# Hybrid DiT step: layer 0's first products by quarters of the contraction, partial sums in SBUF

## The chip, the core and the metric

One core of a Trainium2 chip runs the whole step as one program. Five engines work from their own queues: TensorE (PE in the rows, with its weight loads as PEld), VectorE (DVE), ScalarE (ACT), GpSimd (POOL) and SyncE (SP, which here only issues transfers). Transfers go through 16 DMA engines that all queues share. The metric is the device time of one execution in microseconds.

## What is computed

One inference step of a backbone with two layers, for 128 context tokens and 128 latent tokens (two groups, 256 tokens in all) of 2048 channels, in float32. Cut to what matters here:

```
for each layer:
    sh1, sc1, g1, sh2, sc2, g2 = silu(cond) @ ada_w + ada_b       # 6 x 2048, for both groups
    h = rmsnorm(x, nw0) * (1 + sc1) + sh1
    u = h @ w_in                                                  # 2048 x 5760
    q, k, v, u_hy, u_rkv, w_dn, a_dn, g_dn = split(u)
    att = attention(q, k, v)
    hy  = hyena(short_conv(u_hy))                                 # long convolution
    rw  = rwkv(short_conv(u_rkv), w_dn, a_dn, g_dn)               # bidirectional scans, 12 heads
    x = x + g1 * rmsnorm([att, hy, rw] @ w_out, nw1)
    h = rmsnorm(x, nw2) * (1 + sc2) + sh2
    x = x + g2 * rmsnorm(relu(h @ mlp_w1)**2 @ mlp_w2, nw3)       # 8192 hidden
```

## The kernel before

**Products.** Every float32 product is made of three passes with operands in two float32r parts (hi x hi, lo x hi, hi x lo). `wload` fetches a piece of 128 rows by up to 1024 columns of a weight matrix into a ring `wr` of seven tiles (SP issues), ScalarE casts its high part `wh`, VectorE subtracts for the low part `wl` (three tiles each). `ws` puts output channels on the partitions (256 moving columns, the tokens), `as_` puts tokens on the partitions (512 or 256 moving columns). The contraction has 16 tiles of 128 (k-tiles). Each product accumulates over all of them in one of two PSUM tiles `mm`.

**Modulation.** `ada_group` makes 512 columns of the modulation: eight loads of 512 KB through the same ring `wr`, narrow matmuls (L337), a copy to `arow` on ScalarE, small column sums on PE (L358, or L349 for the gates), and the bias on VectorE. A float32 matmul of the program stands as two in the trace. The groups wait in a list `adaq`; `ada_boot` steps the first two in turn, `ada_step` steps the first one.

**The order.** The program is written by generators, and the framework orders each engine's instructions after that. In the boot (`build`) layer 0's first two modulation vectors come as eight groups, two for each quarter of the channels. When a quarter is modulated, a step of `norm` makes its 512 channels of h in two parts (`acth`, `actl`), and the two products of `mixer_first` (low-rank inputs of the scans, and the first batch's keys) take four k-tiles. The mixer then runs the gate product, the first batch's r and v, the attention's queries, keys and values (three `as_` products), the second batch's keys, r and v, three products for hyena, and the output projection in three phases, each of which takes the channels that are ready. `run` advances `Side` between the k-tiles: the hyena filter, the scans (two batches of three blocks; for each batch three times `rwkv_stage1`, then `rwkv_invert`, `rwkv_stage2` and `rwkv_out`), attention and hyena. Modulation for later goes in at a pace as well. `drain` advances them alone when a phase's channels are not there yet, with a modulation step wherever none of them is due.

**Names in the rows.** `sm` are small PSUM tiles (three), `ada` the modulation's; `osh`, `osl` are the two parts of the mixer's output, `acc` the output projection's sum in SBUF, `rX`, `rXo`, `rdout`, `rXT` the inversion's matrix, its result, that result in DRAM and back in SBUF, `rG`, `rLA` operands of the block scans. L969 and L971 are the block scans' matmuls (L967 and L969 after), L986 and L1033 belong to their outputs.

Of the kernel before, what the change touches and what calls it, by code (L numbers as in the profile page):

```python
# [33 lines left out]
def _shape_constants():  # L34
# [52 lines left out]
    for k, v in c.items():  # L87
# [15 lines left out]
# tile counts by size class and weight slots; then the pace of the work merged into the products  # L103
OPTS = dict(mm_bufs=2, sm_bufs=3, raw=7, hi=3, lo=3, t0=16, t1=8, k1=25, k2=15, k4=19, ada_mix=1.0,
            ada_mlp=0.5, sr=3.5, sq=3, sh=4, so=7, ra=0.3, wa1=1.5, wa2=0.5, w0=1, w1=3, wi=0.5,
            ni=3, w2=0.5, w3=3, w4=2, w5=0.25, fill=8, b1=2, b2=5)
# [3 lines left out]
class Pools:  # L110
    """Tiles of a pool; one without bufs of its own takes a slot of its size's class."""
# [14 lines left out]
class Side:  # L126
    """Work merged into the main stream: generators advanced a few steps at a time.
    A generator yields how many units of the main stream its next step should leave between."""
# [7 lines left out]
    def step(self, n):  # L136
        """Up to n steps of every generator that is ready."""
# [16 lines left out]
class Kern:  # L154
# [52 lines left out]
    def wload(self, src, nk, ncol):  # L207
        """A piece of a weight matrix as two float32r parts, [row in k-tile, k-tile, column]."""
# [51 lines left out]
    def params(self, l):  # L260
        """Per-channel vectors of layer l, channel on the partitions."""
# [29 lines left out]
        # modulation of the two norms: scale and shift, [channel, k-tile, group]  # L291
# [14 lines left out]
        # 0.5*w0, 0.5*a0; 0.5*k_a and 1-0.5*k_a  # L306
# [10 lines left out]
    def ada_group(self, l, P, i, cg, boot):  # L317
        """512 columns of the modulation: k-tiles mod 4 in the array's four column tiles, then their sum."""
# [3 lines left out]
        if i in (2, 5) and cg == 0:  # L322
            # bias and norm weight of the gate's columns, for each column tile
# [22 lines left out]
        if i in (2, 5):  # L346
            # rows 0 and 1 of each column tile: 128 columns for the two groups
# [27 lines left out]
    def ada_boot(self):  # L375
        """A step of one of two groups in turn: the other's tail does not hold the array."""
# [46 lines left out]
    def norm(self, P, parts, isc, ish, act):  # L423
        """Normalised and modulated channels in two float32r parts; a step per 512 channels."""
# [24 lines left out]
    def ws(self, act, w, widths, ps):  # L449
        """Channels out: ps[:w, b, 256] += w[:, block b]^T h; a generator, a step per load."""  # L450
# [3 lines left out]
        for kq in range(KT // nk):  # L454
            hi, lo = self.wload(w[kq * nk * 128:(kq + 1) * nk * 128, :], nk, ncol)
            for kk in range(nk):
                k = kq * nk + kk
                hh, hl = act[k // 4][0][:, k % 4, :], act[k // 4][1][:, k % 4, :]
                c0 = 0
                for b, wd in enumerate(widths):  # L460
                    o = ps[0:wd, b * 256:(b + 1) * 256]
                    h, lw = hi[:, kk, c0:c0 + wd], lo[:, kk, c0:c0 + wd]
                    m = nc.tensor.matmul(o, lhsT=h, rhs=hh, start=(k == 0 and b % 2 == 0), stop=False, skip_group_check=True)  # L463
# [3 lines left out]
                    nc.tensor.matmul(o, lhsT=lw, rhs=hh, start=False, stop=(k == KT - 1), skip_group_check=True)  # L467
# [3 lines left out]
    def as_(self, lhs, ks, w, ncol, ps):  # L471
        """Tokens out: ps[tok, g, ncol] += h_g w over the k-tiles ks; lhs[k] = (hi, lo) [128, 256]."""
# [16 lines left out]
    def conv(self, ps, wv, nb, b, tag, bufs=None):  # L489
        """Width-3 convolution along the tokens of each group; ps [128, 256]."""  # L490
# [9 lines left out]
    def sin_(self, ps, bias, tag):  # L500
        """sin(ps + bias), the argument brought into [-pi, pi]."""
# [836 lines left out]
```

## Time and profile before

| | before |
|---|---|
| median of three runs | 2959.11 us (2955.79 to 2960.27) |
| profiled execution, span from first to last instruction | 2961.5 us |
| PE busy | 2862.3 us, 97% |
| VectorE, ScalarE busy | 56%, 42% |
| DMA | 654.61 MB, mean 221 GB/s |
| mean granted TensorE clock | 0.976 |

The profiled execution has no time of its own beside its span; the span is 2.4 us above the median of the runs. The granted clock is a share of full speed: 1.00 is 2.4 GHz and 0.50 is 1.2 GHz, its two levels; a value between them is a mean over a stretch. A busy PE is not one at its peak, since matmuls overlap and their ends are modelled; rows from the chain of waits are better for prices, because they count the time from one step to the next.

### The profile page before, as it was taken

Reading aid. Unit: us, or ns where it says so; the run is one execution under the profiler, and the core shown is the slowest. Engines: PE = TensorE matmul, PEld = TensorE weight load, DVE = VectorE, ACT = ScalarE, POOL = GpSimd, SP = SyncE. Lnnn points to the kernel's source line nnn. Section 1 sums busy time; section 2 is a strip of 40 time slices with the busy share of each in tenths; the row PEclk is TensorE's granted clock in tenths of the full one; section 3 lists DMA queues with packets and bytes.
Section 4 is the critical chain, followed back from the end, with each engine's and each line's share of the span. In section 5 each row is a group of like instructions: output and inputs, shape, how many; then the busy total and the mean of one; then the engine's idle time right before and its main releaser. Section 6 shows DMA issues by size and latency. Waiting matters only on the chain.

```text
span 2961.5 us, 48597 instructions
## 1 busy us (share of the span) xinstructions
PE 2862.3 (97%) x19435; PEld 2310.5 (78%) x19435; DVE 1649.5 (56%) x2678; ACT 1248.4 (42%) x1904; POOL 194.4 (7%) x392
## 2 busy tenths in 40 slices
PE   6899999999899999999998999999989999999998
PEld 2476788766698897887876878877659989889896
DVE  1246676776654454454446577577666545555455
ACT  2244345433544343343436444453335444444343
POOL 0021201202000000000100111012010000000000
PEclk8789999999999999999999999999989999999999
DMA  8876675477877777777978947545676656666574
GB/s 305 288 229 226 194 222 173 136 242 264 283 242 241 233 239 242 245 240 232 302 250 260 291 153 229 192 141 177 224 253 198 188 189 188 190 189 189 189 242 130
DMA packets 367788, 654.61 MB, mean 221 GB/s; under 512 B 49253, under 2 KB 86830, under 8 KB 367435
## 3 DMA queue, kind: packets, MB, share of 16 engines
q1 hardware_dynamic: 352288, 610.88, 64.1%
q0 software_dynamic: 13696, 36.98, 4.0%
q8 instruction: 152, 2.49, 0.3%
q10 hardware_dynamic: 1579, 3.66, 0.3%
q14 instruction: 73, 0.60, 0.1%
HBM read 632.22 MB, written 19.20 MB: 220 GB/s over the span
## 4 chain that ended last, share of the span: by engine, by line
PE 92%; DMA 3%; DVE 3%; ACT 2%; issue 1%; DVEq 0%; ACTq 0%; SPq 0%
PE mm L463 14%; PE mm L467 13%; PE mm L466 13%; PE mm L482 12%; PE mm L485 11%; PE mm L486 11%; PE ada L337 6%; PE sm L872 2%; DMA wr<-in_ada_w_dram 1%; PE sm L893 1%; PE sm L337 1%; PE sm L971 1%; PE sm L986 1%; DMA wr<-in_w_out_dram 1%; PE ada L358 1%; PE sm L673 1%
## 5 line engine op out<-in xcount | busy, mean ns | idle before, releaser
L216 DVE TENSOR_TENSOR wl<-wr,wh 128x1024 fp32r<-128x1024 f32 (+1 forms) x784 | 928.0, 1185 | 902.5 <-ACT wh L215 874.5
L215 ACT CAST wh<-wr 128x1024 fp32r<-128x1024 f32 (+1 forms) x784 | 797.5, 1020 | 1120.9 <-PE mm L466 521.4
L463 PE MATMUL mm<-acth,wh 128*128 128x256 f32 (+1 forms) x3200 | 916.0, 286 | 5.7 <-ACT acth L444 4.6
L467 PE MATMUL mm<-acth,wl 128*128 128x256 f32 (+1 forms) x3200 | 899.7, 281 | 2.5 <-DVE wl L216 2.5
L466 PE MATMUL mm<-actl,wh 128*128 128x256 f32 (+1 forms) x3200 | 897.9, 281 | 0.1
L463 PEld LDWEIGHTS mm<-acth,wh 128*128 128x128 f32 (+1 forms) x3200 | 601.6, 188 | 87.1 <-issue 62.2
L467 PEld LDWEIGHTS mm<-acth,wl 128*128 128x128 f32 (+1 forms) x3200 | 601.3, 188 | 10.8 <-DVE wl L216 3.7
L466 PEld LDWEIGHTS mm<-actl,wh 128*128 128x128 f32 (+1 forms) x3200 | 601.8, 188 | 3.5 <-issue 2.6
L482 PE MATMUL mm<-wh,fh 128*128 128x512 f32 x1024 | 406.8, 397 | 0.0
L486 PE MATMUL mm<-wh,fl 128*128 128x512 f32 x1024 | 404.7, 395 | 0.0
L485 PE MATMUL mm<-wl,fh 128*128 128x512 f32 x1024 | 401.9, 393 | 0.0
L482 PEld LDWEIGHTS mm<-wh,fh 128*128 128x128 f32 x1024 | 192.2, 188 | 64.3 <-issue 22.2
L486 PEld LDWEIGHTS mm<-wh,fl 128*128 128x128 f32 x1024 | 192.2, 188 | 45.5
L485 PEld LDWEIGHTS mm<-wl,fh 128*128 128x128 f32 x1024 | 192.3, 188 | 44.9
L337 PE MATMUL ada<-wr,cs 128*32 128x512 f32 x1280 | 209.5, 616 | 5.0 <-DMA wr<-in_ada_w_dram 4.2
L482 PE MATMUL mm<-wh,osh 128*128 128x512 f32 x256 | 108.8, 425 | 0.9 <-ACT osh L1140 0.5
L485 PE MATMUL mm<-wl,osh 128*128 128x512 f32 x256 | 103.6, 405 | 3.8 <-DVE wl L216 3.8
L486 PE MATMUL mm<-wh,osl 128*128 128x512 f32 x256 | 101.8, 398 | 0.0
L337 PE MATMUL sm<-wr,cs 128*32 128x512 f32 x256 | 62.7, 727 | 18.0 <-DMA wr<-in_ada_w_dram 17.2
L337 PEld LDWEIGHTS ada<-wr,cs 128*32 128x32 f32 x1280 | 31.9, 109 | 58.2 <-issue 30.0
L482 PE MATMUL mm<-wh,acth 128*128 128x512 f32 (+1 forms) x192 | 75.0, 391 | 0.0
L872 PE MATMUL sm<-rZR,rKB 64*128 64x256 f32 x384 | 72.9, 411 | 0.4 <-ACT rKBt L850 0.4
(323 smaller groups left out, 2667.7 us busy)
## 6 DMA issues: line engine op xcount, KB each, us to landing
wr<-in_mlp_w_dram SPq DMA_DIRECT2D x512, 512.0 KB
wr<-in_ada_w_dram SPq DMA_DIRECT2D x384, 512.0 KB
wr<-in_w_in_dram SPq DMA_DIRECT2D x96, 512.0 KB
wr<-in_w_in_dram SPq DMA_DIRECT2D x112, 384.0 KB
wr<-in_w_out_dram SPq DMA_DIRECT2D x64, 512.0 KB
gb<-gate POOLq DMA_DIRECT2D x16, 512.0 KB, 9.5
xd<-acc SPq DMA_DIRECT2D x24, 256.0 KB
xo<-xd POOLq DMA_DIRECT2D x12, 512.0 KB, 14.1
```

The source lines that it names most:

```text
L215: nc.scalar.copy(hi, raw)
L216: nc.vector.tensor_sub(lo, raw, hi)
L337: m = nc.tensor.matmul(ps[32 * j:32 * j + 32, :], lhsT=self.cs[:, 2 * (kq - 1) + j, :], rhs=w[j // 2][:, j % 2, :], start=(kq == 1), stop= ...
L358: nc.tensor.matmul(pv[:, j, :], lhsT=rows[:, j * 128:(j + 1) * 128], rhs=sel[:, 0:2], start=True, stop=True)
L463: m = nc.tensor.matmul(o, lhsT=h, rhs=hh, start=(k == 0 and b % 2 == 0), stop=False, skip_group_check=True)
L466: nc.tensor.matmul(o, lhsT=h, rhs=hl, start=False, stop=False, skip_group_check=True)
L467: nc.tensor.matmul(o, lhsT=lw, rhs=hh, start=False, stop=(k == KT - 1), skip_group_check=True)
L482: m = nc.tensor.matmul(o, lhsT=hh, rhs=hi[:, kk, :], start=first, stop=False)
L485: nc.tensor.matmul(o, lhsT=hh, rhs=lo[:, kk, :], start=False, stop=False)
L486: nc.tensor.matmul(o, lhsT=hl, rhs=hi[:, kk, :], start=False, stop=last)
L673: nc.tensor.matmul(ps[:, j * nk:(j + 1) * nk], lhsT=qT[o:o + 64, h // 2, :], rhs=kT[o:o + 64, h // 3, :], start=True, stop=True)
L872: nc.tensor.matmul(ps[h][:, i * 256:(i + 1) * 256], lhsT=KB[hs, d, g, i, :], rhs=ZR[hs, d, g, :, :].rearrange("p i t -> p (i t)"), start=T ...
```

## The change

In layer 0 seven products are made by quarters of the contraction: the low-rank inputs, the first batch's keys, r and v, and the attention's two 512-column products and its values. `mixer_first` is now one generator. For each quarter it runs the four k-tiles of each of the seven products into an `mm` tile; `put` copies the first quarter to SBUF tiles (ScalarE) and adds later quarters to them (VectorE). In the boot the modulation of the next quarter is stepped beside it, 1.8 steps per k-tile. The last quarter runs at the start of the mixer. The convolutions and the low-rank step then read SBUF instead of PSUM, and the scans and the attention both start there, beside the gate product. Layer 1 has the same products in the same order as before, without the two products that were started ahead. Hyena's transposes take one PSUM tile at a time instead of two. Comments and docstrings are gone.

```diff
@@ Kern.ws
-    def ws(self, act, w, widths, ps):
+    def ws(self, act, w, widths, ps, ks=range(KT)):
...
-        for kq in range(KT // nk):
-            hi, lo = self.wload(w[kq * nk * 128:(kq + 1) * nk * 128, :], nk, ncol)
+        for k0 in ks[::nk]:
+            hi, lo = self.wload(w[k0 * 128:(k0 + nk) * 128, :], nk, ncol)
...
@@ Kern.mixer_first
         W = self.A["w_in"][l]
-        ps = self.mm(), self.mm()
-        return [(ps[0], self.ws(act, W[:, C_WA:C_WA + 384], [96] * 4, ps[0])),
-                (ps[1], self.ws(act, W[:, C_R + 768:C_R + 768 + 384], [128] * 3, ps[1]))]
+        F = self.F = {n: sb([128, 1024], F32, tag="f" + n) for n in ("wa", "k", "r", "v")}
+        F["qk"] = [sb([128, 1024], F32, tag="aqk") for g in range(2)]
+        F["av"] = [sb([128, 256], F32, tag="av") for g in range(2)]
+        cols = {"wa": (C_WA, [96] * 4), "k": (C_R + 768, [128] * 3), "r": (C_R, [128] * 3), "v": (C_R + 1536, [128] * 3)}
+
+        def put(c, dst, src):
+            if c == 0:
+                nc.scalar.copy(dst, src)
+            else:
+                nc.vector.tensor_add(dst, dst, src)
+
+        for c in range(4):
+            ks = range(4 * c, 4 * c + 4)
+            lhs = {k: (act[c][0][:, k % 4, :], act[c][1][:, k % 4, :]) for k in ks}
+            for n, (c0, widths) in cols.items():
+                ps = self.mm()
+                yield from self.ws(act, W[:, c0:c0 + sum(widths)], widths, ps, ks)
+                w, m = widths[0], 256 * len(widths)
+                put(c, F[n][0:w, 0:m], ps[0:w, 0:m])
+            for c0, n in ((0, 512), (512, 512), (1024, 256)):
+                ps = self.mm()
+                yield from self.as_(lhs, ks, W[:, c0:c0 + n], n, ps)
+                for g in range(2):
+                    put(c, F["qk"][g][:, c0:c0 + n] if c0 < 1024 else F["av"][g][:], ps[:, g * 512:g * 512 + n])
+            yield None
@@ Kern.mixer
+        if first is not None:
+            self.run(first, 1, ada)
+            self.rwkv_lora(self.F["wa"], P)
+            for nm in "krv":
+                rkv_conv(nm, 0, self.F[nm])
+            scans()
+            self.side.add(self.attention(l, P, self.F["qk"], self.F["av"]), self.hyena(l, P, hy), rate=o["ra"])
+            gate()
+        else:
...
@@ Kern.hyena
-        pz = [self.sm(), self.sm()]
...
+            pz = self.sm()
+            for j in range(4):
+                nc.tensor.transpose(pz[:, j * 128:(j + 1) * 128], z[j][:, g, :], self.ident)
...
@@ Kern.build
-        while self.adaq or todo:
-            if self.adaq:
-                self.ada_boot()
+        n = 0
+        while len(self.adaq) > 6:
+            self.ada_boot()
             n += 1
...
-            if cg < 4 and len(self.adaq) < 2 * (4 - cg) - 1:
-                todo.append((n + self.o["b1"], lambda: next(norm)))
-                todo.append((n + self.o["b2"], products))
-                cg += 1
-            while todo and (todo[0][0] <= n or not self.adaq):
-                todo.popleft()[1]()
+        for c in range(4):
+            next(norm)
+            left = 2 * (2 - c) if c < 3 else 0
+            due = 0.0
+            if c < 3:
+                for step in iter(lambda: next(first), None):
+                    due += self.o["bo"]
+                    while due >= 1 and len(self.adaq) > left:
+                        self.ada_boot()
+                        due -= 1
+                while len(self.adaq) > left:
+                    self.ada_boot()
...
-            acc, ss = self.mixer(l, p, act, first)
+            acc, ss = self.mixer(l, p, act, first if l == 0 else None)
```

Three places in the order of the engines. First SP's loads in the boot, where a quarter's modulation meets the products (`in_ada_w_dram` is the modulation's matrix, `in_w_in_dram` that of the products). Before:

```order
L331 DMA wr_297<-in_ada_w_dram 128x2x512
L331 DMA wr_303<-in_ada_w_dram 128x2x512
L331 DMA wr_305<-in_ada_w_dram 128x2x512
L214 DMA wr_307<-in_w_in_dram 128x2x384
L214 DMA wr_337<-in_w_in_dram 128x2x384
L214 DMA wr_367<-in_w_in_dram 128x2x384
L214 DMA wr_391<-in_w_in_dram 128x2x384
L331 DMA wr_415<-in_ada_w_dram 128x2x512
L331 DMA wr_421<-in_ada_w_dram 128x2x512
```

The same place after the change:

```order
L331 DMA wr_437<-in_ada_w_dram 128x2x512
L331 DMA wr_443<-in_ada_w_dram 128x2x512
L331 DMA wr_454<-in_ada_w_dram 128x2x512
L331 DMA wr_456<-in_ada_w_dram 128x2x512
L214 DMA wr_464<-in_w_in_dram 128x2x384
L331 DMA wr_479<-in_ada_w_dram 128x2x512
L214 DMA wr_505<-in_w_in_dram 128x2x384
L331 DMA wr_535<-in_ada_w_dram 128x2x512
L214 DMA wr_539<-in_w_in_dram 128x2x384
L214 DMA wr_563<-in_w_in_dram 128x2x384
L214 DMA wr_589<-in_w_in_dram 128x2x512
L214 DMA wr_607<-in_w_in_dram 128x2x512
```

Where four loads for products stood in one piece between sixteen for modulation, there are now thirteen: those of the first three products (six) spread among the modulation's loads, and those of the other four (seven) almost in a row.

Second VectorE in the boot's second stage after the change (`wl` is a split for the product that follows, `fr` and `fv` are partial sums in SBUF, `mm_896` and `mm_971` the products r and v):

```order
L216 TENSOR_TENSOR wl_974<-wr_972,wh_973 128x768
L1080 TENSOR_TENSOR fr_288<-fr_288,mm_896 128x768
L216 TENSOR_TENSOR wl_998<-wr_996,wh_997 128x768
L442 TENSOR_SCALAR xnt_1139<-sm_1134,mod_11_98,mod_10_97 128x128
L216 TENSOR_TENSOR wl_1024<-wr_1022,wh_1023 128x1024
L445 TENSOR_TENSOR actl_108<-xnt_1139,acth_107 128x4x128
L216 TENSOR_TENSOR wl_1042<-wr_1040,wh_1041 128x1024
L1080 TENSOR_TENSOR fv_289<-fv_289,mm_971 128x768
```

The add of r stands behind a split for v, and the add of v behind two splits for the first attention product. Before, VectorE had no such adds here, and four splits in a row per stage.

Third PE at the end of the output projection's second phase. Before, the scans' matmuls stand between the phase's products (`mm`):

```order
L486 MATMUL mm_6450<-wh_6452,osl_6350 128x512
L969 MATMUL sm_6463<-rG_5217,rLA_5214 32x64
L969 MATMUL sm_6463<-rG_5217,rLA_5213 32x64
L969 MATMUL sm_6463<-rG_5217,rLA_5214 32x64
L969 MATMUL sm_6463<-rG_5217,rLA_5213 32x64
L969 MATMUL sm_6463<-rG_5217,rLA_5214 32x64
L482 MATMUL mm_6450<-wh_6452,osh_6349 128x512
L485 MATMUL mm_6450<-wl_6453,osh_6349 128x512
L486 MATMUL mm_6450<-wh_6452,osl_6350 128x512
```

After, they stand behind the phase's last product, with modulation (`ada`) between them:

```order
L337 MATMUL ada_6509<-wr_6575,cs_71 32x512 x2
L337 MATMUL ada_6509<-wr_6588,cs_71 32x512 x2
L358 MATMUL ada_6509<-const_66,arow_6594 128x2 x4
L337 MATMUL ada_6612<-wr_6613,cs_71 32x512 x2
L969 MATMUL sm_6383<-rG_5337,rXT_6327 32x64
L969 MATMUL sm_6406<-rG_5575,rXT_6327 32x64
L969 MATMUL sm_6425<-rG_5805,rXT_6327 32x64
L337 MATMUL ada_6612<-wr_6626,cs_71 32x512 x2
L969 MATMUL sm_6383<-rG_5337,rXT_6327 32x64 x7
```

From the second phase's last product to the first product of the third phase there are 28 loads' modulation matmuls (56 of L337), the whole of the second batch's block scans and its outputs.

## Rows read from the trace of the kernel before

**Rows 1.** The page: span, busy time, granted clock in 40 slices (tenths).
```profile
span 2961.5 us, 48597 instructions
PE 2862.3 (97%) x19435; PEld 2310.5 (78%) x19435; DVE 1649.5 (56%) x2678; ACT 1248.4 (42%) x1904; POOL 194.4 (7%) x392
...
PEclk8789999999999999999999999999989999999999
```

**Rows 2.** Stretches: length, busy us per engine, granted clock, DMA share, GB/s.
```profile
54.00:90.00 36.00, 30.17 (x173) 17.73 (x174) 8.11 (x17) 7.41 (x14) 0.00 (x0) 0.81 0.79 278
90.00:125.00 35.00, 30.25 (x174) 17.64 (x174) 8.06 (x16) 7.36 (x13) 0.00 (x0) 0.80 0.82 290
125.00:157.00 32.00, 23.44 (x148) 15.90 (x146) 9.28 (x17) 7.68 (x14) 0.00 (x0) 0.81 0.88 295
...
190.00:234.00 44.00, 44.00 (x351) 36.70 (x346) 19.29 (x26) 18.14 (x25) 6.89 (x12) 1.00 0.90 285
234.00:345.00 111.00, 110.70 (x637) 78.58 (x635) 74.40 (x145) 52.39 (x97) 23.04 (x52) 1.00 0.58 183
```

**Rows 3.** The same view inside the second boot stage.
```profile
95.00:100.00 5.00, 5.00 (x45) 5.00 (x44) 0.43 (x1) 0.00 (x0) 0.00 (x0) 1.00 1.04 389
100.00:105.00 5.00, 4.30 (x35) 1.50 (x33) 0.00 (x0) 0.00 (x0) 0.00 (x0) 1.00 0.55 177
...
115.00:120.00 5.00, 5.00 (x19) 3.32 (x20) 0.56 (x2) 0.29 (x1) 0.00 (x0) 0.50 0.60 206
```

**Rows 4.** Boot: a piece of the chain; waits of SP's queue, 54 to 157 us.
```profile
102.62 5.24 DMA wr<-in_ada_w_dram
...
SPq L331 <- PE sm L337: 27.8, 21, 5.9
SPq L214 <- PE sm L337: 27.3, 11, 4.0
```

**Rows 5.** 793 to 1555 us: groups of instructions; the chain by line, one piece.
```profile
L463 PE MATMUL mm<-acth,wh 128*128 128x256 f32 x961 | 271.0, 282 | 0.0
...
L482 PE MATMUL mm<-wh,fh 128*128 128x512 f32 x512 | 205.1, 401 | 0.0
...
by line: PE mm L482 16.4%; PE mm L486 15.7%; PE mm L485 15.5%; PE mm L463 15.5%; PE mm L466 14.7%; PE mm L467 14.7%; PE ada L337 6.5%; PE ada L358 0.8%; PE ada L349 0.2%
...
799.05 1.00 PE ada L337 x8
```

**Rows 6.** Pieces of the chain in the boot, at the lower clock.
```profile
75.70 1.87 PE sm L358 x8
...
118.63 1.06 PE sm L434 x4
```

**Rows 7.** VectorE groups: adds from PSUM 157 to 742 us; splits 54 to 157.
```profile
L1150 DVE TENSOR_TENSOR acc<-acc,mm 128x512 f32<-128x512 f32 x16 | 10.4, 683 | 10.5 <-PE mm L486 10.4
...
L216 DVE TENSOR_TENSOR wl<-wr,wh 128x768 fp32r<-128x768 f32 x15 | 13.9, 954 | 6.0 <-ACT wh L215 5.7
```

**Rows 8.** Inversion steps as a group; from its result to the scans, in time.
```profile
L933 DVE TENSOR_TENSOR rX<-rX,rkt 112x30 f32<-112x30 f32 (+14 forms) x60 | 19.7, 328 | 1.1
...
649.29 3.18 SPq L945 DMA_DIRECT2D rdout<-rXo  x8
...
657.50 0.52 PE L971 MATMUL sm<-rG,rXT 32*32 32x64 f32 x6
```

**Rows 9.** Chain around the third phase's start; copies of the block scans as groups.
```profile
690.25 0.57 PE sm L969 x16
...
708.25 4.67 DMA wr<-in_w_out_dram
...
714.56 1.13 PE sm L1033 x4
...
L977 DVE COPY rG<-sm 32x256 f32<-32x256 f32 x24 | 10.0, 420 | 18.9 <-PE sm L971 18.5
...
L979 ACT COPY rG<-sm 32x256 f32<-32x256 f32 x24 | 8.7, 363 | 29.8 <-DVE rG L977 29.6
```

More of the change, by code (lines that the diff above doesn't have):

```diff
@@ L462, in ws @@
                     h, lw = hi[:, kk, c0:c0 + wd], lo[:, kk, c0:c0 + wd]
-                    m = nc.tensor.matmul(o, lhsT=h, rhs=hh, start=(k == 0 and b % 2 == 0), stop=False, skip_group_check=True)
+                    m = nc.tensor.matmul(o, lhsT=h, rhs=hh, start=(k == ks[0] and b % 2 == 0), stop=False, skip_group_check=True)
                     if b == 0 and kk == 0:
@@ L466, in ws @@
                     nc.tensor.matmul(o, lhsT=h, rhs=hl, start=False, stop=False, skip_group_check=True)
-                    nc.tensor.matmul(o, lhsT=lw, rhs=hh, start=False, stop=(k == KT - 1), skip_group_check=True)
+                    nc.tensor.matmul(o, lhsT=lw, rhs=hh, start=False, stop=(k == ks[-1]), skip_group_check=True)
                     c0 += wd
@@ L1077, in mixer @@
         W = A["w_in"][l]
-        lhs = [(act[k // 4][0][:, k % 4, :], act[k // 4][1][:, k % 4, :]) for k in range(KT)]
         self.rwkv_init()
@@ L1096, in rkv @@
                 rkv_conv(nm, bt, ps)
-        self.run(first[0][1], 1, ada)
-        self.rwkv_lora(first[0][0], P)
-        self.run(first[1][1], 1, ada)
-        rkv_conv("k", 0, first[1][0])
-        ps = self.mm()
-        self.run(self.ws(act, W[:, C_G:C_G + 256], [128] * 2, ps), o["sh"], ada)
-        self.rwkv_gate(ps, P)
-        rkv(0, "rv")
-        self.side.add(self.rwkv_batch(l, P, 0, u), self.rwkv_out(l, P, 0), self.rwkv_batch(l, P, 1, u), self.rwkv_out(l, P, 1))
-        qk = [sb([128, 1024], F32, tag="aqk") for g in range(2)]
@@ L1109, in mixer, with gate @@
-        v = [sb([128, 256], F32, tag="av") for g in range(2)]
-        for c0, n in ((0, 512), (512, 512), (1024, 256)):
-            ps = self.mm()
-            self.run(self.as_(lhs, range(KT), W[:, c0:c0 + n], n, ps), o["sq"], ada)
-            for g in range(2):
-                dst = qk[g][:, c0:c0 + n] if c0 < 1024 else v[g][:]
-                nc.scalar.copy(dst, ps[:, g * 512:g * 512 + n])
-        hy = []
-        self.side.add(self.attention(l, P, qk, v), self.hyena(l, P, hy), rate=self.o["ra"])
+        def gate():
+            ps = self.mm()
+            self.run(self.ws(act, W[:, C_G:C_G + 256], [128] * 2, ps), o["sh"], ada)
+            self.rwkv_gate(ps, P)
@@ new lines, in scans @@
+        def scans():
+            self.side.add(self.rwkv_batch(l, P, 0, u), self.rwkv_out(l, P, 0), self.rwkv_batch(l, P, 1, u), self.rwkv_out(l, P, 1))
+        if first is not None:
[7 more added lines that the diff above has]
+        else:
+            ps = self.mm()
+            self.run(self.ws(act, W[:, C_WA:C_WA + 384], [96] * 4, ps), 1, ada)
+            self.rwkv_lora(ps, P)
+            rkv(0, "k")
+            gate()
+            rkv(0, "rv")
+            scans()
+            lhs = {k: (act[k // 4][0][:, k % 4, :], act[k // 4][1][:, k % 4, :]) for k in range(KT)}
+            qk = [sb([128, 1024], F32, tag="aqk") for g in range(2)]
+            v = [sb([128, 256], F32, tag="av") for g in range(2)]
+            for c0, n in ((0, 512), (512, 512), (1024, 256)):
+                ps = self.mm()
+                self.run(self.as_(lhs, range(KT), W[:, c0:c0 + n], n, ps), o["sq"], ada)
+                for g in range(2):
+                    dst = qk[g][:, c0:c0 + n] if c0 < 1024 else v[g][:]
+                    nc.scalar.copy(dst, ps[:, g * 512:g * 512 + n])
+            self.side.add(self.attention(l, P, qk, v), self.hyena(l, P, hy), rate=o["ra"])
@@ L1259, in build @@
         first = self.mixer_first(0, act)
-        n, cg, todo = 0, 0, deque()
-        def products():
-            for _, g in first:
-                for _ in range(4):
-                    next(g)
-        while self.adaq or todo:
-            if self.adaq:
-                self.ada_boot()
+        n = 0
+        while len(self.adaq) > 6:
+            self.ada_boot()
             n += 1
@@ L1290, in build @@
                     pass
-                first = self.mixer_first(l, act)
-            acc, ss = self.mixer(l, p, act, first)
+            acc, ss = self.mixer(l, p, act, first if l == 0 else None)
             self.ada_until(l, 3)
```

17 lines of the change are left out of this document (7 added, 10 removed).

## The prediction

> **What bounds the kernel now.** I read the page first: TensorE (PE) is busy 97% of 2961.5 us, and its granted clock is full except at the start, around the sub-layer boundaries and in a few slices between [rows 1]. So time can only be won where PE waits or runs at its lower level. Then the stretches [rows 2]: the three boot stages, 54 to 157 us, are the weak place. There PE's mean clock is 0.80 to 0.81, and DMA moves 278 to 295 GB/s. From 190 us on PE is full at clock 1.00. A boot stage cut in pieces of 5 us shows why [rows 3]: with the first products on the array the clock is 1.00 and DMA brings 389 GB/s; then the products run out, PE has only the modulation (narrow matmuls that wait for 512 KB loads), the chain shows one wait of 5.24 us [rows 4], and the clock goes to 0.50 behind it. DMA drops to 177 and 206 GB/s within the same stage, because SP cannot issue into a ring of seven tiles: it waits 27.8 and 27.3 us for the modulation's matmuls to free one [rows 4]. Neither engine is the bound of the stage; they take turns. The profiled execution is 2.4 us above the median of 2959.1; I sum against its 2961.5 and take the difference off the median.
>
> **The price of PE.** From 793 to 1555 us PE never waits: 762 us, of which the chain gives 92.5% to the products and 6.5% to the modulation [rows 5]. The products there are 2884 matmuls of 256 columns (961, 962 and 961 in the three lines, of which one stands) and 1536 of 512 (three lines of 512). Counting a 512 as two, 762 x 0.925 / 5956 = 0.118 us per 256 columns. Eight modulation matmuls take 1.00 us [rows 5].
>
> **What moves.** Full products, in matmuls of 256 columns: r 144, v 144, two attention products of 512 columns 192 each, the attention values 96: 768. Three quarters, 576, go from behind the boot into it: 576 x 0.118 = **68 us** less behind 157 us. There they stood at full clock with PE full between 190 and 345 us [rows 2], so they are worth that price and hardly more. Low-rank inputs and the first keys already lay three quarters in the boot.
>
> **What a boot stage becomes.** Products: (192 + 144 + 768) / 4 = 276 matmuls, 32.6 us (before: 84, 9.9 us). Modulation: two groups, 64 trace matmuls, 8.0 us. The 16 small column sums and 16 transposes cost 1.87 us per eight and 1.06 us per four at the lower level [rows 6], 7.9 us, so about 4 us at the upper. Sum **44.6 us** of PE at 2.4 GHz, where now 21.9 us of work takes (157 - 54) / 3 = 34.3 us. DMA per stage: 16 modulation loads of 0.524 MB and 512 rows x 2816 columns x 4 bytes = 5.77 MB, 14.2 MB in all. The row that is most like this (products with modulation between, 190 to 234 us) moves 285 GB/s at a DMA share of 0.90 with PE 44.00 of 44.00 us busy [rows 2]. At its rate the stage takes 49.7 us; scaled to a full share, 317 GB/s, 44.7 us. So both engines now bound the stage at nearly the same time. Bounds: 45 us if each covers the other's waits, 55.4 us if the mean clock stays at 0.805. I take **49 us**, by the nearest row: 3 x 49 - 103 = **+44 us**.
>
> **The partial sums.** Seven products a quarter now leave PSUM each: 5888 columns, 11.5 pieces of 512. On VectorE such an add takes 683 ns [rows 7]: 7.9 us per later quarter; the first quarter's are plain copies on ScalarE. I cost them at nothing in the boot: VectorE's splits of the stage's weights come to 11264 / 768 x 0.954 = 14.0 us [rows 7], about 4 us of modulation and norm come on top, 26 us of 49; and VectorE's order puts each add behind the splits of the next product, so PE has its weights by then. What hides them is the other of the two PSUM buffers. With that cover gone they cost up to 7.9 us a stage. The last quarter runs in the mixer with seven short products where there were two: 0 to 7.9 us, **+2** taken.
>
> **The scans get less cover.** They start beside the gate product instead of the attention products, and the second batch's block scans now stand in a drain, behind phase 2 of the output projection. PE's order shows no product there, only modulation and scan matmuls. Before the block scans comes the end of the inversion: 12 of its 30 steps stand behind the last split on VectorE, two operations of 0.328 us each [rows 8], 7.9 us, and the copies; then stores and loads through DRAM, 8.2 us from the first store's issue to the first scan matmul [rows 8]. Against these 16 to 18 us PE has 2.8 us left of the last product and one modulation group, 5 us: some 10 us idle. In the block scans PE has 21 rounds of 0.57 us [rows 9] and two modulation groups between them, enough to be full. The output norms behind it made PE wait from 708.25 to 714.56 us, 6.3 us, partly for a load [rows 9]; now modulation fills most of that, 2 us idle remain. So 12 against 6.3: **+7 us** rounded up. Bounds: 0, and +23 if the rounds of the three blocks do not overlap (21 x (0.57 + 0.42 + 0.36) = 28 us, the last two from the scan's copies on VectorE and ScalarE [rows 9], against 12 us of PE). Queued behind SP's wait for the inversion's result are modulation loads only. The modulation done in the drain is missing from the feed-forward part later, so it is no cost. Hyena's transposes in two halves and layer 1's unrolled order change no matmul count: 0.
>
> **Sum:** -68 + 44 + 2 + 7 = -15 us; 2961.5 - 15 = 2946.5, or **2944 us** against the median.
>
> **A rule that speaks against it.** In this trace the clock fell to 0.50 behind a wait of 5.24 us for a load with little work around it [rows 3, 4], and stayed at 1.00 where products and modulation alternate [rows 2]. The Trainium skill, "TensorE: Matmul & The Clock Gate", section "Why this matters for your kernels", advises for thin products (M under 512; here 256 tokens) to run all k-tiles in one go before waiting for data, since otherwise the clock oscillates from k-tile to k-tile. This change does the opposite; by that rule the second rival below holds, by the row the sum above. No run here yet shows which.
>
> **The rivals.**
> 1. *Both bounds met.* Stages of 45 us and a hidden drain: -68 + 32 + 2 + 0 to 7 = -34 to -27, 2925 to 2932 us. For it: PE is gapless in the 190 to 234 us row. Against: a stage has two unequal parts, first three products with all 16 modulation loads (10.7 MB, so DMA leads), then four products with few loads, and seven tiles of ring are little to even that out. 0.19.
> 2. *The boot's clock stays low (slower).* In the first part of each stage, 120 product matmuls, 8 us of modulation and 4 us of small work, 26 us at the upper level, PE still waits for loads as it does now. If half of that runs at 1.2 GHz, a stage takes 49 + 13 = 62 us: +83, sum +24, 2983 us; if all of it, 75 us and 3022 us. It decides from a stage of 54 us on (3 x 54 - 103 + 9 = 68). For it: 0.80 to 0.81 in all three stages now. Against: PE has three times the product work to put under each wait. 0.19.
> 3. *No change:* the won time goes back in the drain. Its upper bound, +23, gives -68 + 44 + 2 + 23 = +1, 2960 us. For it: the scans' matmuls to the end of phase 2 are the same, but 16 x 24 = 384 product matmuls (45 us) fewer lie beside them. Against: the drain has three modulation groups to run. 0.17.
> The forecast itself, 2935 to 2953 us: 0.45.
>
> **How the numbers follow.** About 0.2% (6 us) is what a measurement of this kernel can tell from no change. Faster by more (under 2953): the forecast and rival 1, 0.64. Within: rival 3, 0.17. Slower: rival 2, 0.19. The range of 8 in 10 goes from 2925 (rival 1's bound) to 2972 (rival 3 and the mild end of rival 2). The forecast's own range is 2932 to 2955.
>
> **What would show it.** Right: three stages of 47 to 51 us with a granted clock of at least 0.95 and 280 GB/s or more; the last quarter modulated near 201 us instead of 157; layer 0's feed-forward part starting some 15 us earlier than 766 us; everything behind it shifted, not changed. Wrong: stages over 54 us, a clock near 0.8 in them, PE waiting in the boot for an add or for loads, or over 20 us of idle PE between phases 2 and 3 of the output projection. The sum fails first if the stage length is off, since it counts three times.

## The result: 31 us slower, not 15 us faster

The changed kernel takes **2990.4 us** (2982.7 to 2998.8, four runs) against 2959.2 us: a ratio of 1.0106, with an interval of 1.0091 to 1.0121. The forecast was 2944 us, its range ended at 2972. The profiled execution, from which the rows come, spans 2996.5 us, the longest of the four, and stands 35.0 us above the one of before [rows 1].

Counted from instants in the two traces, the 35 us come about like this (before, after, in us; where nothing else is said, a stage begins with its first matmul on TensorE):

| | before | after | difference, running |
|---|---|---|---|
| third boot stage ends | 157.5 | 200.8 | +43.3 |
| first product of the last quarter | 157.5 | 209.9 | +52.4 |
| scans' first step (keys' inverse norms) | 247.1 | 267.3 | +20.2 |
| scans' last output | 718.0 | 743.2 | +25.2 |
| layer 0's feed-forward part starts | 765.8 | 796.9 | +31.1 |
| its last product ends | 1555.2 | 1589.8 | +34.6 |
| layer 1's first product | 1573.4 | 1614.8 | +41.4 |
| layer 1's feed-forward part starts | 2228.4 | 2263.3 | +34.9 |
| end | 2961.5 | 2996.5 | +35.0 |

So layer 0 up to its feed-forward part has 31 of the 35 us; of the rest, 3.5 us come in the feed-forward part and 6.8 at the boundary behind it, and 6.5 go again in layer 1's mixer. The boot costs 43 us up to the last product of its third stage, as forecast (44); up to the first product of the last quarter, with which the third stage ended before, it costs 52. The stretch behind it, from which 576 matmuls were taken, got shorter by 12 us, or by 21 from that first product on, where the forecast had 68 less 9. The rows of the scans tell it another way: they start 20 us later, take 5 us more, and behind their last output 6 us more pass to the feed-forward part.

### The profile page after: what moved, and what is told of

It is laid out like the page before. It is cut to its first block, busy times and chain, and to the rows that moved or that the text cites. A ratio compares the mean times of both kernels' runs of the same rounds, so it can differ in the third digit from the quotient of the medians.

```text
span 2996.5 us, 48669 instructions
## 1 busy us (share of the span) xinstructions
PE 2868.4 (96%) x19435; PEld 2317.4 (77%) x19435; DVE 1670.5 (56%) x2708; ACT 1254.0 (42%) x1909; POOL 195.1 (7%) x392
## 5 line engine op out<-in xcount | busy, mean ns | idle before, releaser
L337 PE MATMUL ada<-wr,cs 128*32 128x512 f32 x1280 | 215.5, 625 | 23.3 <-DMA wr<-in_ada_w_dram 19.7
L337 PEld LDWEIGHTS ada<-wr,cs 128*32 128x32 f32 x1280 | 32.7, 110 | 76.0 <-issue 33.1
L482 PEld LDWEIGHTS mm<-wh,osh 128*128 128x128 f32 x256 | 49.1, 192 | 34.1 <-issue 16.5
```

The lines of the kernel that those rows point to most:

```text
L337: m = nc.tensor.matmul(ps[32 * j:32 * j + 32, :], lhsT=self.cs[:, 2 * (kq - 1) + j, :], rhs=w[j // 2][:, j % 2, :], start=(kq == 1), stop= ...
L482: m = nc.tensor.matmul(o, lhsT=hh, rhs=hi[:, kk, :], start=first, stop=False)
```

## The profile after

The page: the span, TensorE's busy time, and its busy share and granted clock in 40 slices of 75 us (tenths).

```profile
span 2996.5 us, 48669 instructions
PE 2868.4 (96%) x19435; PEld 2317.4 (77%) x19435; DVE 1670.5 (56%) x2708; ACT 1254.0 (42%) x1909; POOL 195.1 (7%) x392
PE   6999999997899999999998999999998999999998
PEclk8999999997899999999998999999998999999999
```

The two low slices from 674 to 824 us stand out in both rows. The view of stretches shows the boot and then the mixer with its end (the columns are those of [rows 2]); phase 2's last product ends at 667.7 us, phase 3's first begins at 744.6 us.

```profile
54.00:90.00 36.00, 35.13 (x244) 25.70 (x245) 12.14 (x19) 14.04 (x20) 0.00 (x0) 1.00 0.95 329
90.00:125.00 35.00, 32.91 (x215) 22.51 (x213) 10.17 (x13) 9.90 (x16) 0.00 (x0) 1.00 0.84 278
125.00:157.00 32.00, 31.92 (x213) 26.56 (x210) 19.73 (x28) 12.36 (x17) 0.00 (x0) 1.00 0.73 229
157.00:190.00 33.00, 31.46 (x206) 22.87 (x205) 15.47 (x21) 10.73 (x15) 0.00 (x0) 0.95 0.97 340
...
201.00:252.00 51.00, 46.33 (x281) 34.51 (x280) 33.70 (x60) 30.46 (x44) 11.59 (x21) 0.93 0.82 249
252.00:520.00 268.00, 263.02 (x2203) 212.35 (x2202) 183.73 (x421) 120.21 (x258) 33.34 (x70) 0.97 0.59 186
520.00:668.00 148.00, 143.07 (x699) 98.99 (x702) 106.65 (x227) 58.39 (x104) 23.96 (x53) 0.98 0.51 166
668.00:691.00 23.00, 6.61 (x47) 2.24 (x40) 4.90 (x14) 0.59 (x1) 4.43 (x9) 0.71 0.88 276
691.00:745.00 54.00, 48.82 (x543) 29.23 (x541) 24.17 (x62) 13.37 (x31) 8.19 (x14) 0.84 0.82 258
745.00:797.00 52.00, 40.81 (x181) 23.76 (x180) 33.04 (x58) 25.26 (x56) 5.97 (x11) 0.84 0.76 256
```

The same view of the kernel before, for the stretch that answers to the last six rows:

```profile
157.00:247.00 90.00, 87.68 (x609) 70.09 (x609) 42.58 (x64) 42.70 (x60) 16.35 (x29) 0.95 0.79 253
247.00:520.00 273.00, 271.25 (x2167) 212.61 (x2167) 189.26 (x423) 129.72 (x268) 37.65 (x75) 1.00 0.62 193
520.00:700.00 180.00, 177.83 (x1252) 129.16 (x1252) 130.34 (x277) 67.34 (x123) 23.49 (x55) 1.00 0.63 204
700.00:709.00 9.00, 9.00 (x110) 7.17 (x109) 6.15 (x17) 2.40 (x6) 4.70 (x8) 1.00 0.80 264
709.00:766.00 57.00, 49.01 (x247) 28.25 (x244) 37.07 (x77) 30.35 (x69) 9.64 (x19) 0.94 0.90 290
```

A useful way to read them is busy time times clock: what is missing to the length of a row is time that TensorE lost (an estimate, since the clock is a mean over the row). Without the first row of each, before, 519 us lose 15 (1.8 + 2.2 + 0 + 10.9); after, 545 us lose 70 (12.9 + 7.8 + 18.3 + 13.0 + 17.7). With it, 609 us lose 22 and 596 us lose 78. The work left is 69 us less, as the forecast took 68 us out of the mixer; but 56 us of it came back as idle time and low clock. 31 of these lie in the drain behind phase 2, the others are spread over the rest.

The timeline of the drain, on the queues and TensorE:

```profile
673.39 3.72 SPq L943 DMA_DIRECT2D rdout<-rXo  x8
673.67 2.31 POOL L184 DMA_DIRECT2D gb<-gate  x4 [0.30 <-PE ada L337]
675.99 0.53 POOL L184 DMA_DIRECT2D xo<-in_x_prompt_dram  x1
...
680.91 0.39 SPq L951 DMA_DIRECT2D rXT<-rdout  x1
681.34 4.39 SPq L331 DMA_DIRECT2D wr<-in_ada_w_dram  x1
...
685.90 0.56 SPq L951 DMA_DIRECT2D rXT<-rdout  x1
...
690.77 0.84 PE L969 MATMUL sm<-rG,rXT 32*32 32x64 f32 x6 [14.14 <-DMA rXT<-rdout]
```

The inversion's result is stored from 673.39 us, and TensorE gets it back at 690.77: 17.4 us where it took 8.2 [rows 8]. Eight loads of 512 KB (`gb`, `xo`, the residual's) are issued from 673.67 us on, seven of them within 4 us. In two runs further down that have the same eight loads right behind the store, half the modulation and earlier scans, the way took 17.3 and 18.2 us; in the run with modulation earlier, where they come 5.6 us behind it, 9.0; in the control, with none of them, 6.3. TensorE's waits between 667 and 745 us:

```profile
PE sm L969 <- DMA rXT<-rdout: 14.1, 1, 14.1
PE ada L358 <- ACT arow L343: 3.2, 2, 2.6
PE ada L337 <- DMA wr<-in_ada_w_dram: 2.0, 2, 1.2
```

Of the 77 us gap the rest is work: the second batch's block scans and outputs, and 56 modulation matmuls (28 loads). In the kernel before all this lay beside products.

## The experiments

Two theories were open. Cover means work on TensorE under which another wait does not show. In theory 1 the scans lost their cover: their steps have latency, and with fewer products beside them it shows. In theory 2 the modulation's 0.5 MB loads lost theirs. In a third, which came with the first runs, scans at a faster pace make TensorE wait within the products that are left. The gap behind phase 2 is the time from that phase's last product to the first of phase 3. The times of all runs stand at the end of this section.

**Pace.** The scans' steps stand at a pace beside the products; a faster one moves the second batch back beside phase 2.

```diff
-... sr=3.5, sq=3, sh=4, ... w1=3, wi=0.5, ... w3=3, w4=2, ...
+... sr=6, sq=3, sh=6, ... w1=2, wi=0.25, ... w3=2, w4=1, ...
```

> The changed kernel with a faster pace of the scans (both rates from 3.5 and 4 to 6, the three gaps that the program leaves for the inversion's transfers from 3, 3 and 2 units to 2, 2 and 1, and from 0.5 to 0.25 between pieces of the inversion). The second batch's block scans then stand beside the products of phase 2 again, and the drain between phases 2 and 3 is empty; the modulation that ran in it (56 matmuls, 28 loads) goes behind phase 3 instead (68 matmuls there, 20 in the changed kernel, 32 in the kernel before). Theory 1, the drain cost 77 us because the scans lost their cover: the gap behind phase 2 falls from 76.9 us to under 12, the gap behind phase 3 stays near 21, time 2925 to 2945 us. Theory 2, the modulation's loads lost their cover: the gap behind phase 2 falls too, but the one behind phase 3 grows by 24 loads of 0.524 MB at some 300 GB/s, 42 us, to about 63; time 2960 to 2975 us. Theory 3, scans at this pace make TensorE wait within the products: hyena's and the output projection's products get longer by 30 us or more in sum, time over 2975 us.

3010.6 us. The gap behind phase 2 is gone, the feed-forward part starts at 794.1 us, 2.8 earlier. The loads moved behind phase 3, where the DMA engines are full (last row, a share of 0.96):

```profile
253.00:520.00 267.00, 253.56 (x2080) 202.50 (x2078) 184.15 (x433) 117.71 (x263) 38.57 (x84) 0.97 0.52 163
520.00:742.00 222.00, 211.91 (x1387) 151.50 (x1386) 150.68 (x306) 80.15 (x145) 33.76 (x69) 0.94 0.62 201
742.00:794.00 52.00, 39.40 (x193) 11.93 (x192) 17.11 (x44) 15.99 (x42) 1.24 (x2) 0.86 0.96 340
```

52 us instead of 21: this is theory 2's case in kind. The time is theory 3's (over 2975 us), and so is a part of the loss: the first two rows lose 44 us, where the changed kernel lost 21 from 252 to 668 us. The options hold for both layers, and layer 1's mixer took 677 us instead of 648.5; without these 29 us the run would stand near 2982 us (an estimate from the two).

**Modulation earlier, and none in the drain.**

```diff
-        ada = o["ada_mix"]
+        ada = o["ada_mix"] * (1.45 if l == 0 else 1)
@@ drain
-                if self.adaq:
-                    self.ada_step(1)
-                    self.side.now += 0.2
-                else:
-                    self.side.now = min(e[1] for e in self.side.q)
+                self.side.now = min(e[1] for e in self.side.q)
```

> The changed kernel with layer 0's modulation stepped 1.45 times as often beside the mixer's products, and no modulation in the drain: the scans run there alone. Theory 1, latency of the scans is the price: the gap behind phase 2 stays at 45 to 60 us (the end of the inversion 5 us, 8.2 us through DRAM, 28 us of block scans, some 10 us of outputs), and the gap behind phase 3 stays near 21; time 2965 to 2985 us. Theory 2, the modulation's loads are the price: without them the gap behind phase 2 falls to 25 us or less; time 2935 to 2950 us.

2982.4 us, feed-forward part at 788.5 us. The gap falls to 25.6 us, as theory 2 has it, the time is theory 1's (2965 to 2985 us): phase 2's last product ends at 710.8 us instead of 667.7. What left the gap went into the products' stretches.

**Both.**

> The changed kernel with both: the faster pace of the scans and layer 0's modulation stepped 1.45 times as often beside the mixer's products. Nothing is left in the drain and 20 modulation matmuls behind phase 3. Theories 1 and 2 together (scans and modulation both lost their cover, and can find it beside the products that are left): gap behind phase 2 under 12 us, behind phase 3 some 21 us, time 2915 to 2940 us. Theory 3, the products left are too little cover and TensorE waits within them instead: 2960 us or more.

3014.9 us; less layer 1's 35 us (684 instead of 648.5) about 2980 us. Nothing lies in the drain, and still the feed-forward part starts at 790.1 us, only 6.8 earlier: theory 3's side. A new wait stands ahead of phase 3, at 726 to 740 us:

```profile
PE mm L482 <- ACT osh L1176: 13.1, 1, 13.1
```

`osh` stands on ScalarE behind casts of weights, of which the timeline shows the first and the last. They waited for their loads, while the residual's loads were on the same DMA engines:

```profile
728.44 1.05 ACT L215 CAST wh<-wr 128x1024 fp32r<-128x1024 f32 x1 [11.85 <-DMA wr<-in_w_out_dram]
...
738.94 1.04 ACT L215 CAST wh<-wr 128x1024 fp32r<-128x1024 f32 x1 [5.70 <-DMA wr<-in_w_out_dram]
...
739.89 1.32 ACT L1176 CAST osh<-o 128x256 fp32r<-128x256 f32 x4
```

**Less moved.** Only low-rank inputs, k, r and v by quarters; the attention's products behind the scans' start, as before.

```diff
-            for c0, n in ((0, 512), (512, 512), (1024, 256)):
...
-            self.side.add(self.attention(l, P, self.F["qk"], self.F["av"]), self.hyena(l, P, hy), rate=o["ra"])
             gate()
         else:
...
+        if True:
             lhs = {k: ...
```

> The changed kernel with only the low-rank inputs, keys, r and v by quarters; the attention's three products stand behind the start of the scans again, as in the kernel before. 360 matmuls of 256 columns (42 us) go back behind the boot. Theories 1 and 2 (cover): the gap behind phase 2 is under 12 us, boot stages are 36 to 41 us; against the kernel before 216 matmuls (25 us) leave the mixer and the boot grows by 5 to 19 us, so the time is 2938 to 2953 us. If instead the scans' start beside the gate product were at fault, with cover or without: over 2965 us.

2960.6 us, the same as before (1.0005, 0.9992 to 1.0019) and 1% less than the changed kernel; it lies between the two forecasts, and neither is met. The third boot stage ends 39.6 us earlier than in the changed kernel (161.2 us), and the stretch behind it, with the 42 us of attention products back in it, is only 15 us longer: the feed-forward part starts at 772.3 us, 24.6 earlier. The gap ahead of phase 3 is 14.5 us, the one behind it 32.3.

**Which of the two.** First the changed kernel without half of layer 0's modulation (that of its second norm), then without the inversion's steps:

```diff
-            self.ada_push(l, p, (2, 4, 3, 5) if l == 0 else (4, 3, 5))
+            self.ada_push(l, p, (2,) if l == 0 else (4, 3, 5))
...
```

> The changed kernel without layer 0's modulation for its second norm: 8 of 16 groups (64 loads of 0.524 MB) are left out, the norm takes the first norm's vectors, and the gate of the feed-forward part comes after the mixer. The drain between phases 2 and 3 and the boundary behind phase 3 so hold almost no modulation. Some 24 us of TensorE's own work go with it. Theory 1, the chain of the scans (475 us from its first step at 267 us to its last output at 743 us) sets the end of the mixer: the gap behind phase 2 stays over 40 us, and the feed-forward part starts at 765 us or later (797 us in the changed kernel), time over 2960 us. Theory 2, the modulation's loads without cover set it: the gap behind phase 2 falls under 20 us, idle time and low clock between 253 us and the feed-forward part fall from 65 us to 25 us, it starts at 735 us or before, time under 2935 us.

2964.8 us; the feed-forward part starts at 766.6 us, and the gap is still 68.6 us. All three of theory 1's numbers, none of theory 2's. In stretches (phase 2 ends at 652.9 us, the block scans begin at 687.3):

```profile
653.00:687.00 34.00, 10.66 (x24) 1.08 (x24) 15.54 (x40) 0.95 (x1) 6.56 (x12) 0.57 0.84 257
687.00:721.00 34.00, 31.44 (x434) 26.00 (x436) 16.34 (x41) 5.86 (x17) 3.71 (x6) 0.65 0.26 72
```

In the first row TensorE waits 13.6 us for the inversion's result, which comes through DRAM, and 10.9 us for loads of the little modulation that is left. With DMA at 72 GB/s the second row cannot wait for loads: it is the scans' own chain, and TensorE, 92% busy with it, has a clock of 0.65.

The second cut, of the inversion's steps:

```diff
         for k in range(1, 31):
-            n = 31 - k
...
-            nc.vector.tensor_add(X[:, 0:k, k + 1:], X[:, 0:k, k + 1:], tv)
             if k % ni == 0:
```

> The changed kernel without the 30 steps of the scans' inversion in both batches and layers (60 VectorE operations a batch, 20 us of work that take 49 and 42 us in layer 0); every other instruction and their order on TensorE stay. Theory 1 (scan chain sets the end): layer 0's feed-forward part starts 25 us or more earlier than 797 us. Theory 2 (modulation loads): the loads still lie in the drain, it starts at 785 us or later.

2971.3 us; the feed-forward part starts at 776.7 us, 20.2 earlier: short of theory 1's 25, past theory 2's 12. Counted from the end of the third boot stage, which came 3.0 us earlier, it is 17.2. The gap is 52.7 us. The same cut in the kernel before:

> The kernel before without the 30 steps of the inversion (the same cut as made in the changed kernel, where the feed-forward part then started 20 us earlier). If TensorE's products set the end of the mixer here: the feed-forward part starts within 6 us of 766 us. If the scans' chain already set it before the change: 15 us or more earlier.

2954.5 us, feed-forward part at 763.8 us: 2.0 earlier, and nothing counted from the end of the boot (154.1 us). Before the change the inversion's time was covered; after it, it costs.

**Start of the scans.** In the changed kernel the scans' first step (the keys' inverse norms) is at 267.3 us, 20.2 us later than before.

```diff
...
-            self.run(first, 1, ada)
+            self.run(iter(lambda: next(first), None), 1, ada)
...
             scans()
+            self.run(first, o["sq"], ada)
```

> The changed kernel with the scans started before the last quarter of the attention's three products, not behind it: 120 matmuls, 14 us, stand behind the start instead of ahead of it. Theory 1: the scans' first step comes 14 us earlier, their last output too, and the feed-forward part starts at 780 to 788 us; time 2975 to 2983 us. Theory 2: the start of the feed-forward part stays within 5 us of 797 us.

The first step came at 250.8 us, 16.5 earlier, and the last output 14.5 us later, at 757.6 us; the feed-forward part started at 802.8 us. Theory 1 in the form that the scans run a fixed 470 us from their start falls, and neither theory's forecast is met. (The time of 2982.8 us is less than the changed kernel's all the same, as layer 1's mixer took 642 us.) The drain kept its modulation and lost even more, 36 us:

```profile
681.00:755.00 74.00, 55.45 (x559) 33.72 (x556) 22.35 (x57) 11.81 (x27) 14.01 (x26) 0.68 0.73 236
```

**What the 576 matmuls are worth.** The kernel before, with half of layer 0's modulation left out as a control, and then without the matmuls as well; the pace and the places of all else stay.

> A control for the next run: the kernel before, without layer 0's modulation for its second norm (8 of 16 groups left out, the norm takes the first norm's vectors, the gate of the feed-forward part comes after the mixer). TensorE is busy in the mixer as it was, so the feed-forward part starts earlier by the 24 us of TensorE's own work in these groups and by part of the 24 us boundary: 730 to 742 us instead of 766.

> As the control, and layer 0's r, v and the attention's three products are made from the last quarter of the contraction alone: the 576 matmuls that the change moves into the boot are simply not there, everything else stays in its place. The forecast's price for them, 0.118 us each: the feed-forward part starts 68 us earlier than in the control. Theory 1, the scans' latency is hidden by products and they run some 470 us whatever lies beside them: r and v are done 25 us earlier, so the scans start 25 us earlier and the feed-forward part too, by 20 to 40 us; over 25 us of idle time and low clock appear in the mixer that the control does not have.

```diff
         for kq in range(KT // nk):
+            if kq * nk < skip:
+                for _ in range(nk):
+                    yield 3 * 256 * len(widths)
+                continue
...
```

2938.0 and 2900.5 us, two executions each; the feed-forward part starts at 745.3 and 710.2 us: **35 us** for the 576 matmuls, 38 counted from the end of the boot (146.6 and 149.6 us), not 68. Stretches of the control from the scans' first step on:

```profile
237.00:520.00 283.00, 281.54 (x2250) 232.05 (x2248) 207.98 (x460) 139.69 (x289) 42.94 (x89) 1.00 0.51 152
520.00:639.00 119.00, 110.52 (x495) 85.41 (x493) 85.28 (x177) 43.36 (x77) 13.99 (x32) 0.83 0.39 120
639.00:745.00 106.00, 82.88 (x686) 60.73 (x685) 70.45 (x136) 42.40 (x89) 17.11 (x32) 0.86 0.59 187
```

And of the one without the matmuls:

```profile
209.00:520.00 311.00, 292.40 (x2208) 238.49 (x2207) 219.55 (x490) 138.34 (x299) 46.70 (x101) 0.92 0.42 126
520.00:604.00 84.00, 78.38 (x350) 61.86 (x348) 65.11 (x137) 34.42 (x57) 7.78 (x17) 0.88 0.48 147
604.00:710.00 106.00, 83.25 (x685) 60.74 (x685) 69.83 (x134) 41.91 (x86) 17.19 (x32) 0.86 0.58 186
```

Busy time times clock leaves 63 us lost in the first and 91 in the second: 28 us of what was taken out stay as idle time and low clock. The DMA engines have room in both. This is the failed term measured by itself, in a kernel with half of the modulation.

The two starts tell more. Counted from the end of the boot, the scans' first step comes 31.7 us earlier without the matmuls (59.1 us behind it instead of 90.8), and from that step to the feed-forward part it takes 501.5 us instead of 507.9. So r and v, whose 216 matmuls (25 us at the price) stand ahead of the scans' start, brought their price and 6 us more; the attention's 360 (42 us), which lie beside the scans, brought 6.

**A version that might beat both.** Less moved, modulation 1.25 times as often in layer 0, and the residual's loads ahead of phase 2.

```diff
-            if ph == 2:
+            if ph == 1:
                 self.residual_load(P, 2)
```

> The kernel with only low-rank inputs, keys, r and v by quarters (attention's products behind the start of the scans), with layer 0's modulation stepped 1.25 times as often beside the mixer's products and the residual's loads (4.2 MB) placed ahead of phase 2 instead of phase 3. Without the last two the feed-forward part started at 772 us, with 14.5 us of gap ahead of phase 3 and 32 us behind it, against 9 and 24 us before. Theory 2: both gaps get shorter by 15 to 20 us in sum, feed-forward start 752 to 757 us, time 2938 to 2948 us. Theory 1: the scans end at the same 681 us as there and the phases behind them are not shortened, time 2955 us or more.

The feed-forward part starts at 750.9 us, 14.9 before that of the kernel before, but the time is 2964.6 us: layer 1's mixer took 662 us, with 37 us without a product at 2110 to 2147 us. So the loads early in layer 0 alone (`ph == (2 if l else 1)`):

> Low-rank inputs, keys, r and v by quarters, the attention's products behind the start of the scans, layer 0's modulation 1.25 times as often, and the residual's loads ahead of phase 2 in layer 0 alone. With these loads early in both layers the feed-forward part of layer 0 started at 751 us, 15 us before that of the kernel before, but layer 1's mixer took 662 us against 645 to 655. If the loads in layer 1 were the reason: layer 1's mixer takes 645 to 655 us and the time is 2940 to 2950 us, less than both kernels. If not: 2955 us or more.

2961.9 us: no change from before, 1% less than the changed kernel. The hole of 37 us is gone, the feed-forward part of layer 0 starts at 752.2 us, yet layer 1's mixer, whose code is that of the changed kernel again, still took 658 us. Why it takes 642 to 658 us with the same work in it, from one version of layer 0 to the next, stays open. No run was faster than the kernel before with all of its work done.

| run | median us | ratio to before (interval) | layer 0's feed-forward part starts, us |
|---|---|---|---|
| pace | 3010.6 | 1.0178 (1.0158 to 1.0199) | 794.1 |
| modulation earlier | 2982.4 | 1.0082 (1.0061 to 1.0103) | 788.5 |
| both | 3014.9 | 1.0191 (1.0170 to 1.0212) | 790.1 |
| less moved | 2960.6 | 1.0005 (0.9992 to 1.0019) | 772.3 |
| half the modulation | 2964.8 | 1.0027 (1.0014 to 1.0040) | 766.6 |
| no inversion | 2971.3 | 1.0044 (1.0030 to 1.0057) | 776.7 |
| earlier scans | 2982.8 | 1.0083 (1.0062 to 1.0103) | 802.8 |
| less moved, loads early | 2964.6 | 1.0028 (1.0017 to 1.0039) | 750.9 |
| before, half the modulation | 2938.0 | 0.9929 (0.9903 to 0.9955) | 745.3 |
| the same without the 576 | 2900.5 | 0.9803 (0.9773 to 0.9832) | 710.2 |
| before, no inversion | 2954.5 | 0.9987 (0.9974 to 1.0000) | 763.8 |
| less moved, loads early in layer 0 | 2961.9 | 1.0010 (0.9997 to 1.0023) | 752.2 |

## Why the prediction was wrong

**The boot was right in its stages, and 8 us short at its end.** Stages of 48.2, 50.2 and 50.0 us (49 forecast), 148.4 in sum; as the first begins 1.7 us earlier than before, the third ends 43.3 us later (+44). The clock is 1.00, 1.00, 1.00 and 0.95 over four stretches. The rates are 329, 278, 229 and 340 GB/s, so the 280 failed in two rows. No wait for an add appears. But the last quarter's first product, with which the third stage ended before, now comes 9.1 us behind it: +52.4, where the forecast had +44 and 2 for that quarter. Rival 2 is out: a granted clock of 0.95 to 1.00 stands beside four k-tiles at a time, with modulation in the 1.8 to 3.6 us between the first products of a stage (TensorE idles 4.6 of 136 us). The Trainium skill's rule for thin products ("TensorE: Matmul & The Clock Gate", "Why this matters for your kernels"), by which the clock would oscillate there, did not show.

**The failed step is "There they stood at full clock with PE full between 190 and 345 us [rows 2], so they are worth that price and hardly more."** The 576 matmuls were worth 38 us, not 68, measured with half of the modulation. TensorE was full from 190 to 345 us [rows 2], but it was not alone in setting the pace: from 247 us on the scans lay beside its products with nearly no slack. Two cuts bound this. Without the inversion's steps the kernel before gains 2 us at most, since products fill the time; without the products it gains little more than half, most of it (32 of 38 us) ahead of the scans' start, since the scans fill the rest (their first step to their last output: 463 us, 470 in the control). After the change the first cut brings 17 to 20 us. With all of the modulation the split by place is not measured; there "less moved" took r's and v's 216 matmuls alone out, and from the last quarter's first product to the feed-forward part it took 606.8 us, where the kernel before took 608.3.

**The drain was named and mis-sized.** +7 us in the sum (its own terms, 12 against 6.3, give 5.7), up to +23 in rival 3; TensorE lost 31 us in it (the gap is 76.9 us, where 9.2 had been). The forecast had 12 us of idle time there and no loss by the clock; the rows from 668 to 745 us show 21.6 us idle, 14.1 of them in one wait, and some 10 us by a clock of 0.71 and 0.84. The DRAM round trip was taken as 8.2 us from [rows 8] and took 17.4; "Queued behind SP's wait for the inversion's result are modulation loads only" overlooked POOL's eight residual loads on the same DMA engines. No modulation filled this wait: the timeline shows none on TensorE between 676.6 us and the scan matmul at 690.77.

**"The modulation done in the drain is missing from the feed-forward part later, so it is no cost" failed too.** The feed-forward part holds as many modulation matmuls as before (408 in the trace, 412 before); what lies in the drain is missing beside the mixer's products. Leaving half of layer 0's modulation out brings 9.6 us before and 29.3 us after, both counted from the end of the boot, though the matmuls are the same: some 20 us for modulation with less cover. That cover is the reason is argued from where it lies; the four runs show the 20 us.

Together, from the end of the boot to the feed-forward part: -38 (the matmuls' worth), +20 (modulation), +6 (what remains: the changed kernel with half the modulation takes 566.8 us there, the kernel before without matmuls and with half the modulation 560.6), -12 in all; with the boot's +43, +31 us. Each number is a difference of single profiled executions, good to a few us. Of the 6, 7.7 are the time between the boot and the last quarter's first product in the run with half the modulation (9.1 in the changed kernel, TensorE with modulation and a wait of 4.6 us for a load); without them -1.5 is left.

What stays open is which resource sets the scans' length at a given cover: from their first step to their last output it was 440 us at the faster pace, 471 us in the kernel before, 476 in the changed one, 507 with the earlier start.

## What to carry to other kernels

A stretch in which TensorE is full tells what bounds it now, not what its work is worth when it is taken away: ask how long the other chain in that stretch (here the scans through VectorE and DRAM) would take alone, and price the removed work by the smaller of the two gains. Here work ahead of that chain's start counted in full, and work beside it hardly at all. To measure it, leave the work out and keep all else in place, before moving it. And work that hides under products (narrow modulation matmuls, small scan matmuls) is no cover for other latency: when products leave, count everything that they covered, on every queue.

## What the runs showed of the hardware

Busy is not clock. In the drain of the run with half the modulation the granted clock was 0.50 behind the wait of 13.6 us, came to 1.00, and fell to 0.50 again while TensorE was busy with scan matmuls, 4.87 and 5.00 of 5 us in the last two rows:

```profile
703.00:708.00 5.00, 3.93 (x114) 3.36 (x112) 4.40 (x12) 1.16 (x4) 0.00 (x0) 1.00 0.01 2
708.00:713.00 5.00, 4.87 (x43) 4.48 (x37) 2.51 (x7) 1.52 (x6) 1.26 (x3) 0.62 0.05 11
713.00:718.00 5.00, 5.00 (x36) 4.76 (x35) 1.67 (x5) 0.91 (x3) 1.63 (x3) 0.50 0.15 44
```

With products among them, 237 to 520 us of the control, it was 1.00. A small transfer through DRAM pays for what is queued with it: 8.2 us from store to use before and 6.3 in the control; 17.4, 17.3 and 18.2 us in the three runs in which another queue issued eight loads of 512 KB from under a microsecond behind the store on.
